# Nine of the 22 gate and up tiles of a feed-forward block from seven quarter products, with the high and low half of the input in one matmul

## The chip, the cores and the metric

The kernel runs on one core of a Trainium2 chip. The metric is the device time of one execution in microseconds (us); a kernel's time is the median of its runs. A core has a matrix engine (PE, with its weight loads shown apart as PEld), three other compute engines (DVE, ACT, POOL) and a queue that issues transfers (SP). Each engine runs its instructions in the order in which the program lists them, and waits for the results of others by semaphores.

## The reference, cut to what matters

Two layers, each a feed-forward block, a mixing block (convolution, a recurrent mixer, retention, attention) and a second feed-forward block; 512 tokens of width 1024, a hidden width of 2816. All is fp32.

```python
def swiglu(x, w_gate, w_up, w_down):
    return (jax.nn.silu(x @ w_gate) * (x @ w_up)) @ w_down

for l in range(DEPTH):                                   # DEPTH = 2
    x = x + 0.5 * swiglu(rmsnorm(x, ffn1_norm[l]), ffn1_w_gate[l], ffn1_w_up[l], ffn1_w_down[l])
    h = rmsnorm(x, mix_norm[l])
    ...                                                  # mixers on h @ w_in[l]
    x = x + jnp.concatenate([...], axis=-1) @ w_out[l]
    x = x + 0.5 * swiglu(rmsnorm(x, ffn2_norm[l]), ffn2_w_gate[l], ffn2_w_up[l], ffn2_w_down[l])
return rmsnorm(x, final_norm)
```

So there are four feed-forward blocks. The change touches their `x @ w_gate` and `x @ w_up`.

## The kernel before

Activations lie transposed: `x[d]` is a tile of 128 features by 512 tokens, for d = 0 to 7. An fp32 product is made of three reduced-precision ones (fp32r): each operand is split into a high part and a low part, and `mm3` (L336 to 340) adds high weight by high input (L338), high weight by low input (L339) and low weight by high input (L340). `norm_part` (L258) makes the two parts of the scaled input, `xg`: one tile of 128 x 2 x 512 for each d, high part first.

`ffn` (L343) goes through the hidden width in two halves of 11 tiles of 128. For each tile f it loads the gate and the up weights in one transfer of 1 MB into `w_raw` (a ring of two buffers), splits each of the two into `w_hi` (an ACT copy, L327) and `w_lo` (a DVE subtraction, L328), and makes two accumulations of 24 matmuls of 512 columns: `pg` (gate) and `pu` (up). `w_hi` and `w_lo` are rings of two buffers each, so that in steady work one is read by the gate matmuls and the other by the up matmuls, and a split can begin only when the matmuls that read the older content of its buffer are done. Behind the matmuls come, on other engines, `s = pg * rb` (DVE, L369), the silu (ACT, L370), `g = pu * s` (DVE, L372) and the split of g (ACT L374, DVE L375). After 11 tiles the down projection of that half follows, d = 0 to 7, with 33 matmuls each into `pd`.

PSUM has eight banks under three tags: `mm` (three: `pg` and others), `b` (three: `pu` and others) and `a` (two). The SBUF tiles of 512 columns have tag `f` (23 buffers), those of twice that tag `v` (19).

The order of the work on each engine is made when the program is built, by a list scheduler that follows a model of the engines' times: where several instructions of an engine could go, the one with the higher priority goes first, and priority is the place in the program. `split` runs under `high_priority(offset=AHEAD)`, which puts its instructions 4000 places ahead of where they stand.

Of the kernel before, what the change touches and what calls it, by code (L numbers as in the profile page):

```python
# [23 lines left out]
HALF = NF // 2  # L24
W = 256
AHEAD = 4000
PIECE = 512
MLA_TAGS = (("mm", "mm", "mm"), ("mm", "mm", "mm"), ("b", "a", "mm"), ("b", "a", "mm"))
H = 4
N = 64  # L30
C = 64
# [103 lines left out]
class K:  # L135
# [17 lines left out]
    def setup(self):  # L153
        tc, nc, I = self.tc, self.nc, self.I
        e = self.ctx.enter_context
        self.per = e(tc.tile_pool(name="per", bufs=1))
        self.ring = e(tc.tile_pool(name="ring", bufs=2))
        self.tmp = e(tc.tile_pool(name="tmp", bufs=2))
        self.psp = e(tc.tile_pool(name="ps", bufs=2, space=bass.MemoryType.PSUM))
        self.dr = e(tc.tile_pool(name="dr", bufs=2, space=bass.MemoryType.DRAM))  # L160
        per = self.per
        self.vec = per.tile([P, _vec_layout()], F32, name="vec")
        nc.sync.dma_start(self.vec, I["vec"])

        warm = self.tmp.tile([P, 1], F32, name="warm", bufs=1)
        nc.vector.memset(warm, 0.0)
        nc.scalar.activation(warm, warm, AF.Copy, scale=1.0)
        self.x = [self.ft(f"x{d}") for d in range(KD)]
        first = self.ring.tile([P, 2048], F32, name="w_raw", tag="w_raw", bufs=2)
        self.first = first  # L170
        for d in range(KD):
            nc.sync.dma_start(self.x[d], I["xT"][:, d, :])
            if d in (0, 3):
                q = 512 * (d // 3)
                nc.sync.dma_start(first[:, q:q + 512], I["gu1"][0, 0][:, q:q + 512])
        nc.sync.dma_start(first[:, 1024:2048], I["gu1"][0, 0][:, 1024:2048])
        self.con_t = per.tile([P, I["con"].shape[1]], F32, name="con_t")
        nc.sync.dma_start(self.con_t, I["con"])
        self.rc = per.tile([P, T], F32, name="rc")
        self.rs = per.tile([P, T], F32, name="rs")  # L180
        self.mt = per.tile([P, T], F32, name="mt")
# [76 lines left out]
    def norm_part(self, d, gain, l, square=True):  # L258

        nc, V, A = self.nc, self.nc.vector, self.nc.scalar  # L260
        x = self.x[d]
        if d == 0:
            self.acc = self.ft("acc")
            self.xh, self.xl, self.xo = [], [], []
        if gain == "final_norm":
            self.norm_square(d, True)
            o = self.ft("o")
            A.activation(o, x, AF.Copy, scale=self.v(gain, 0, d))
            self.xo.append(o)
            return  # L270
        hl = self.ht(f"xg{d}", dt=F32R)
        g = self.v(gain, l, d)
        A.activation(hl[:, 0], x, AF.Copy, scale=g)
        V.scalar_tensor_tensor(hl[:, 1], x, g, hl[:, 0].bitcast(F32), ALU.mult, ALU.subtract)  # L274
        self.xh.append(hl[:, 0])
        self.xl.append(hl[:, 1])
        if square:
            self.norm_square(d)
# [61 lines left out]
        T_.matmul(ps, lo, xh, start=False, stop=stop)  # L340


    def ffn(self, l, which, then, between=None):  # L343
        nc, V, A = self.nc, self.nc.vector, self.nc.scalar
        wgu, wdn = self.I[f"gu{which}"], self.I[f"dn{which}"]
        for half in range(2):
            gh, gl = [], []
            for f in range(HALF):
                raw, self.first = self.first, None
# [24 lines left out]
                A.copy(hl[:, 0], g)  # L374
                V.tensor_tensor(hl[:, 1], g, hl[:, 0].bitcast(F32), ALU.subtract)  # L375
                gh.append(hl[:, 0])
                gl.append(hl[:, 1])
            if between is not None:
                between()
                between = None  # L380
            for d in range(KD):
                raw = self.load(wdn[l, half, d], HALF * P)
                pd = self.ps("pd", "a")
                for a, b in ((0, 6), (6, HALF)):
                    hi, lo = self.split(raw[:, P * a:P * b], P * (b - a))
# [27 lines left out]
class Mixers:  # L413
# [44 lines left out]

    def x_back(self):
        k = self.k  # L460
        for d in range(0, KD, 2):
# [304 lines left out]
    def mla(self, j):  # L766
# [29 lines left out]

        po = k.ps("m_po", MLA_TAGS[2 * j + 1][2])

# [477 lines left out]
```

## Time and profile before

| | us |
|---|---|
| median of 3 runs | 2169.64 (2166.54 to 2171.83) |
| the profiled execution | 2169.86 |
| its span, first to last instruction | 2168.1 |
| PE busy in it | 2131.3 (98%) |
| DVE busy | 1113.3 (51%) |
| ACT busy | 711.6 (33%) |
| mean granted PE clock | 0.995 |

Busy times of PE overlap: matmuls are pipelined, and one that is shown with 390 ns starts 227 ns after the one before. What a matmul costs is therefore read from the distance of two starts, not from its length. "Idle before" a group, and what ended it, say who waited for whom.

### The profile page before, as it was taken

To read this page: it belongs to the slowest core of one execution; us is meant where nothing else is said; L and a number is where in the kernel's file an instruction comes from. 1 tells how busy PE (TensorE), PEld (TensorE's weight loads), DVE (VectorE), ACT (ScalarE), POOL (GpSimd) and SP (SyncE) were. 2 spreads that over 40 slices of the span, in tenths; PEclk is the share of its full clock that TensorE was granted. 3 is DMA by queue.
4 is the path that set the end of the run, shared out by engine and by line. 5 is a ranking of instruction groups with operands and counts; after the bars stand their busy time and mean duration, and the time that the engine had idled before them with its cause. 6 is when DMAs were issued, how large, how long until landed. Compare 5 with 4: busy or idle time off the path is not lost.

```text
span 2168.1 us, 27576 instructions
## 1 busy us (share of the span) xinstructions
PE 2131.3 (98%) x11316; PEld 1714.9 (79%) x11316; DVE 1113.3 (51%) x1917; ACT 711.6 (33%) x1061; POOL 122.4 (6%) x146
## 2 busy tenths in 40 slices
PE   8999999999999999999999999999999999999997
PEld 7888888788666888888888888887886578888886
DVE  4454445676577543443544444457756865434433
ACT  4222223443233422222322222335323243222232
POOL 2000001000020100000100000010001210000001
PEclk9999999999999999999999999999999999999998
DMA  4223224144002322322322232242330122223222
GB/s 170 97 85 106 98 95 151 61 118 129 20 21 86 116 98 85 117 97 79 106 97 91 94 109 95 92 147 72 116 101 21 64 90 105 91 80 111 97 87 79
DMA packets 65294, 204.68 MB, mean 94 GB/s; under 512 B 26512, under 2 KB 26768, under 8 KB 50960
## 3 DMA queue, kind: packets, MB, share of 16 engines
q1 hardware_dynamic: 65168, 202.93, 28.5%
q8 instruction: 88, 1.44, 0.3%
q14 instruction: 38, 0.31, 0.0%
HBM read 191.37 MB, written 9.44 MB: 93 GB/s over the span
## 4 chain that ended last, share of the span: by engine, by line
PE 93%; DVE 4%; ACT 1%; DMA 1%; issue 1%; SPq 0%; DVEq 0%; ACTq 0%
PE pg L338 7%; PE pg L340 7%; PE pg L339 7%; PE pu L338 7%; PE pd L340 7%; PE pu L339 7%; PE pd L339 7%; PE pd L338 7%; PE pu L340 7%; PE pj L338 4%; PE pj L339 4%; PE pj L340 4%; PE po L338 1%; PE po L339 1%; PE po L340 1%; PE m_pq L758 1%
## 5 line engine op out<-in xcount | busy, mean ns | idle before, releaser
L327 ACT CAST w_hi<-w_raw 128x1024 fp32r<-128x1024 f32 (+4 forms) x446 | 367.4, 836 | 1132.1 <-PE pg L339 308.9
L328 DVE TENSOR_TENSOR w_lo<-w_raw,w_hi 128x1024 fp32r<-128x1024 f32 (+4 forms) x446 | 425.7, 962 | 229.4 <-ACT w_hi L327 220.1
L338 PE MATMUL pg<-xg,w_hi 128*128 128x512 f32 x704 | 275.5, 391 | 6.2 <-ACT w_hi L327 6.2
L340 PE MATMUL pg<-xg,w_lo 128*128 128x512 f32 x704 | 275.0, 391 | 0.0
L339 PE MATMUL pg<-xg,w_hi 128*128 128x512 f32 x704 | 274.9, 390 | 0.0
L338 PE MATMUL pu<-xg,w_hi 128*128 128x512 f32 x704 | 274.1, 389 | 0.4 <-ACT w_hi L327 0.4
L339 PE MATMUL pu<-xg,w_hi 128*128 128x512 f32 x704 | 274.2, 389 | 0.0
L340 PE MATMUL pu<-xg,w_lo 128*128 128x512 f32 x704 | 273.9, 389 | 0.0
L340 PE MATMUL pd<-g,w_lo 128*128 128x512 f32 x704 | 273.9, 389 | 0.0
L338 PE MATMUL pd<-g,w_hi 128*128 128x512 f32 x704 | 273.9, 389 | 0.0
L339 PE MATMUL pd<-g,w_hi 128*128 128x512 f32 x704 | 273.9, 389 | 0.0
L372 DVE TENSOR_TENSOR g<-pu,s 128x512 f32<-128x512 f32 x88 | 60.9, 692 | 274.0 <-PE pu L340 271.2
L369 DVE TENSOR_TENSOR s<-pg,rb 128x512 f32<-128x512 f32 x88 | 60.8, 691 | 206.5 <-PE pg L340 206.4
L338 PEld LDWEIGHTS pg<-xg,w_hi 128*128 128x128 f32 x704 | 132.7, 188 | 33.7 <-ACT w_hi L327 6.2
L340 PEld LDWEIGHTS pg<-xg,w_lo 128*128 128x128 f32 x704 | 132.7, 188 | 28.5 <-DVE w_lo L328 1.0
L339 PEld LDWEIGHTS pg<-xg,w_hi 128*128 128x128 f32 x704 | 132.7, 188 | 28.0 <-DVE xg L274 0.5
L338 PEld LDWEIGHTS pu<-xg,w_hi 128*128 128x128 f32 x704 | 132.2, 188 | 28.1 <-ACT w_hi L327 0.9
L340 PEld LDWEIGHTS pu<-xg,w_lo 128*128 128x128 f32 x704 | 132.2, 188 | 27.5 <-DVE w_lo L328 0.2
L339 PEld LDWEIGHTS pd<-g,w_hi 128*128 128x128 f32 x704 | 132.2, 188 | 27.5
L338 PEld LDWEIGHTS pd<-g,w_hi 128*128 128x128 f32 x704 | 132.2, 188 | 27.4
L340 PEld LDWEIGHTS pd<-g,w_lo 128*128 128x128 f32 x704 | 132.2, 188 | 27.4
L339 PEld LDWEIGHTS pu<-xg,w_hi 128*128 128x128 f32 x704 | 132.2, 188 | 27.3
(294 smaller groups left out, 2706.5 us busy)
## 6 DMA issues: line engine op xcount, KB each, us to landing
w_raw<-gu SPq DMA_DIRECT2D x87, 1024.0 KB, 4.8
w_raw<-dn SPq DMA_DIRECT2D x64, 704.0 KB, 4.2
w_raw<-win SPq DMA_DIRECT2D x22, 1024.0 KB, 5.1
w_raw<-wo SPq DMA_DIRECT2D x32, 256.0 KB, 2.8
xs<-x SPq DMA_DIRECT2D x16, 256.0 KB, 4.7
x<-xs SPq DMA_DIRECT2D x16, 256.0 KB, 5.7
w_raw<-wtv SPq DMA_DIRECT2D x4, 576.0 KB, 4.2
x<-xT SPq DMA_DIRECT2D x8, 256.0 KB, 5.9
```

The costliest lines, as they stand in the source:

```text
L327: self.split_hi = self.nc.scalar.copy(hi[:, s], raw[:, s])
L328: self.nc.vector.tensor_tensor(lo[:, s], raw[:, s], hi[:, s].bitcast(F32), ALU.subtract)
L338: T_.matmul(ps, hi, xh, start=start, stop=False)
L339: T_.matmul(ps, hi, xl, start=False, stop=False)
L340: T_.matmul(ps, lo, xh, start=False, stop=stop)
L369: V.tensor_tensor(s, pg, rb, ALU.mult)
L372: V.tensor_tensor(g, pu, s, ALU.mult)
L758: mm(pq, wq[i][:, P * h:P * h + P], qa[i], start=i == 0, stop=i == 2)
```

## The change

Nine of the 22 gate and up tiles of each block (f = 3, 5, 7, 9 of the first half, f = 1, 3, 5, 7, 9 of the second; 36 tiles in all) are computed by a new function `seven`. It takes the pair of gate and up weights as a 2 x 2 block matrix (rows: gate or up; columns: the first and the last four of the eight feature tiles) and the input as another (the same feature halves by the first and the last 256 tokens), and forms the product from seven products of quarters instead of eight (the Winograd form of Strassen's method). Each quarter product is four feature tiles by 256 tokens. In it one matmul of 512 columns takes the high weight by the high and the low input side by side (two runs of 256 columns, into the two halves of a bank), and one of 256 columns takes the low weight by the high input into the first half; the two halves are added later.

What is new around it: `sums` makes the four input sums `T` once for each block, behind tile 0 (per pair of feature tiles two ACT copies, four DVE sums, and a split of each); `seven` makes the weight sums on DVE and splits seven quarters instead of four; three PSUM banks are used for the seven products (`y` takes four of them, `z` two, `x` one), with four ACT copies (`taken`) that read out partial results between the products; the combination is made on DVE. The weights arrive in three transfers instead of one. The other 13 tiles of a block, the down projection and the mixers stay.

```diff
+SEVEN = ((3, 5, 7, 9), (1, 3, 5, 7, 9))
+    def sums(self):
+        V, A = self.nc.vector, self.nc.scalar
+        ...
+        for i in range(KD // 2):
+            b = []
+            for d in (i, i + KD // 2):
+                t = self.ft("t_b")
+                A.activation(t, self.x[d], AF.Copy, scale=self.v(gain, l, d))
+                b.append((t[:, 0:256], t[:, 256:512]))
+            (b11, b12), (b21, b22) = b
+            ...
+            V.tensor_tensor(T1, b12, b11, ALU.subtract)
+            V.scalar_tensor_tensor(T2, b22, -1.0, T1, ALU.mult, ALU.subtract)
+            V.scalar_tensor_tensor(T3, b22, -1.0, b12, ALU.mult, ALU.subtract)
+            V.tensor_tensor(T4, T2, b21, ALU.add)
+            ...
+                for q in range(2):
+                    a = t[:, 256 * q:256 * q + 256]
+                    A.copy(hl[q][:, 0], a)
+                    V.tensor_tensor(hl[q][:, 1], a, hl[q][:, 0].bitcast(F32), ALU.subtract)
+
+    def seven(self, src, rb):
+        ...
+        raw = self.ring.tile([P, 2048], F32, name="w_raw", tag="w_raw", bufs=2)
+        nc.sync.dma_start(raw[:, 0:Q], src[:, 0:Q])
+        nc.sync.dma_start(raw[:, Q:3 * Q], src[:, 2 * Q:4 * Q])
+        nc.sync.dma_start(raw[:, 3 * Q:4 * Q], src[:, Q:2 * Q])
+        w22, w12 = raw[:, 2 * Q:3 * Q], raw[:, 3 * Q:4 * Q]
+        def parts(*srcs):
+            hi = self.ring.tile([P, 1152], F32R, name="w_hi", tag="w_hi", bufs=2)
+            lo = self.ring.tile([P, 1152], F32R, name="w_lo", tag="w_lo", bufs=2)
+            ...
+                A.copy(hi[:, z], t)
+                V.tensor_tensor(lo[:, z], t, hi[:, z].bitcast(F32), ALU.subtract)
+        with self.tc.high_priority(offset=AHEAD):
+            w11, = parts(raw[:, 0:Q])
+            V.tensor_tensor(raw[:, 0:2 * Q], raw[:, 0:2 * Q], raw[:, Q:3 * Q], ALU.subtract)
+            r2, r4 = self.ft("w_s2"), self.ft("w_s4")
+            V.scalar_tensor_tensor(r2, raw[:, 0:Q], -1.0, w22, ALU.mult, ALU.subtract)
+            V.tensor_tensor(r4, w12, r2, ALU.add)
+            S1, S2 = parts(raw[:, Q:2 * Q], r2)
+            S4, S3 = parts(r4, raw[:, 0:Q])
+            w22, w12 = parts(raw[:, 2 * Q:4 * Q])
+        y, x, z = self.ps("f_y", "mm"), self.ps("f_x", "b"), self.ps("f_z", "b")
+        ...
+        def product(ps, w, b, start):
+            hi, lo = w
+            for i in range(4):
+                c = slice(P * i, P * i + P)
+                nc.tensor.matmul(ps.rearrange("p (q t) -> p q t", q=2), hi[:, c], b[i], start=start and i == 0,
+                                 stop=False, skip_group_check=True)
+                nc.tensor.matmul(ps[:, 0:256], lo[:, c], b[i][:, 0], start=False, stop=i == 3, skip_group_check=True)
+        def taken(ps):
+            t = self.ft("f_m")
+            A.copy(t, ps)
+            return t
+        product(y, w11, tok(0, 0), True)
+        m1 = taken(y)
+        product(z, S1, T(1), True)
+        m5 = taken(z)
+        product(y, S2, T(2), False)
+        u2 = taken(y)
+        product(z, S4, tok(1, 1), False)
+        product(y, S3, T(3), False)
+        u3 = taken(y)
+        product(x, w12, tok(1, 0), True)
+        product(y, w22, T(4), False)
+        ...                                  # the combination: 9 DVE operations, a silu and a copy on ACT
     def ffn(self, l, which, then, between=None):
         ...
             for f in range(HALF):
+                if f in SEVEN[half]:
+                    g = self.seven(wgu[l, half * HALF + f], rb)
+                    ...                      # the split of g, as in the other tiles
+                    continue
         ...
+                if f == 0 and half == 0:
+                    self.sums()
```

## Rows read from the trace of the kernel before

**Rows 1.** The page, engines: busy time, share, instructions; the chain that ended last.

```profile
PE 2131.3 (98%) x11316; PEld 1714.9 (79%) x11316; DVE 1113.3 (51%) x1917; ACT 711.6 (33%) x1061; POOL 122.4 (6%) x146
PE 93%; DVE 4%; ACT 1%; DMA 1%; issue 1%; SPq 0%; DVEq 0%; ACTq 0%
```

**Rows 2.** Groups by line and shape: busy us, mean ns; idle before, releaser.

```profile
L338 PE MATMUL pg<-xg,w_hi 128*128 128x512 f32 x704 | 275.5, 391 | 6.2 <-ACT w_hi L327 6.2
...
L328 DVE TENSOR_TENSOR w_lo<-w_raw,w_hi 128x1024 fp32r<-128x1024 f32 x174 | 215.1, 1236 | 74.8 <-ACT w_hi L327 65.7
...
L639 DVE TENSOR_TENSOR ret_ms<-ret_ps,ret_big 128x256 f32<-128x256 f32 x32 | 11.5, 418 | 0.1
...
L1100 ACT COPY ch<-psT 128x256 f32<-128x256 f32 x28 | 9.8, 373 | 39.6 <-PE psT L1099 31.4 <-DVE sm L783 3.9 <-PE m_ptp L793 3.3
...
L794 ACT COPY m_pT<-m_ptp 128x512 f32<-128x512 f32 x16 | 9.4, 587 | 8.4 <-PE m_ptp L793 8.4
```

**Rows 3.** Timeline of PE, first matmuls of two neighbouring gate and up tiles.

```profile
98.73 0.39 PE L338 MATMUL pg<-xg,w_hi 128*128 128x512 f32 x1
98.95 0.39 PE L339 MATMUL pg<-xg,w_hi 128*128 128x512 f32 x1
...
109.61 0.39 PE L338 MATMUL pg<-xg,w_hi 128*128 128x512 f32 x1
```

**Rows 4.** Timeline of PE in a projection with 256 columns.

```profile
416.28 0.28 PE L502 MATMUL pn<-w_hi,xg 128*128 128x256 f32 x1
416.40 0.28 PE L503 MATMUL pn<-w_lo,xg 128*128 128x256 f32 x1
416.52 0.28 PE L504 MATMUL pn<-w_hi,xg 128*128 128x256 f32 x1
```

**Rows 5.** Timeline at a tile's end: its last matmuls, then ACT and DVE.

```profile
109.15 0.39 PE L339 MATMUL pu<-xg,w_hi 128*128 128x512 f32 x1
...
109.64 1.05 ACT L327 CAST w_hi<-w_raw 128x1024 fp32r<-128x1024 f32 x1 [3.87 <-PE pu L339]
...
109.88 0.69 DVE L372 TENSOR_TENSOR g<-pu,s 128x512 f32<-128x512 f32 x1 [3.38 <-PE pu L340]
...
110.60 0.62 ACT L374 CAST g<-g 128x512 fp32r<-128x512 f32 x1
...
110.72 1.23 DVE L328 TENSOR_TENSOR w_lo<-w_raw,w_hi 128x1024 fp32r<-128x1024 f32 x1
```

**Rows 6.** Timeline where splits and a PSUM copy compete for ACT.

```profile
491.68 0.39 PE L340 MATMUL pj<-xg,w_lo 128*128 128x512 f32 x1
491.88 1.14 ACT L327 CAST w_hi<-w_raw 128x512 fp32r<-128x512 f32 x2 [3.01 <-PE pj L339]
...
492.93 0.58 ACT L572 COPY ro_r<-pj 128x512 f32<-128x512 f32 x1
```

**Rows 7.** Timeline of PE between two links of the recurrent chain (zy).

```profile
602.52 0.55 PE L793 MATMUL m_ptp<-con_t,m_p 128*128 128x128 f32 x3
...
603.00 0.78 PE L1123 MATMUL zy<-ch,Gm 128*64 128x64 f32 x16
```

**Rows 8.** Timeline: the end of an ACT operation and the matmul that waited for it.

```profile
613.88 0.19 ACT L786 ACTIVATION_READ_ACCUMULATOR m_p<-m_sc,sm,m_fqa 128x1 f32 x1
...
614.13 0.44 PE L793 MATMUL m_ptp<-con_t,m_p 128*128 128x128 f32 x2 [0.17 <-ACT m_p L786]
```

**Rows 9.** Busy time by stretch: one gate and up tile; a stretch of the mixers.

```profile
98.73:109.61 10.88, 10.88 (x50) 9.01 (x48) 4.44 (x5) 3.17 (x4) 0.00 (x0) 1.00 0.29 96
...
595.00:610.00 15.00, 14.27 (x153) 10.39 (x152) 11.10 (x28) 7.52 (x17) 2.12 (x4) 1.00 0.01 2
```

(The columns: PE, PEld, DVE, ACT, POOL busy us with instruction counts, granted clock, DMA share, GB/s.)

**Rows 10.** DMA issues: count, KB of each, median us to landing.

```profile
w_raw<-gu SPq DMA_DIRECT2D x87, 1024.0 KB, 4.8
...
w_raw<-wo SPq DMA_DIRECT2D x32, 256.0 KB, 2.8
```

**Rows 11.** Timeline of PE in the kernel's first matmuls.

```profile
9.42 0.63 PE L338 MATMUL pg<-xg,w_hi 128*128 128x512 f32 x1
9.85 0.63 PE L339 MATMUL pg<-xg,w_hi 128*128 128x512 f32 x1
```

More of the change, by code (lines that the diff above doesn't have):

```diff
@@ L168, in setup @@
         self.x = [self.ft(f"x{d}") for d in range(KD)]
+        self.x_moved = False
         first = self.ring.tile([P, 2048], F32, name="w_raw", tag="w_raw", bufs=2)
@@ L263, in norm_part @@
             self.acc = self.ft("acc")
-            self.xh, self.xl, self.xo = [], [], []
+            self.xh, self.xl, self.xo, self.xhl = [], [], [], []
+            self.gain = (gain, l)
         if gain == "final_norm":
@@ L274, in norm_part @@
         V.scalar_tensor_tensor(hl[:, 1], x, g, hl[:, 0].bitcast(F32), ALU.mult, ALU.subtract)
+        self.xhl.append(hl)
         self.xh.append(hl[:, 0])
@@ L340, in mm3 @@
         T_.matmul(ps, lo, xh, start=False, stop=stop)
+    def sums(self):
+        V, A = self.nc.vector, self.nc.scalar
+        self.T = []
+        gain, l = self.gain
+        for i in range(KD // 2):
[5 more added lines that the diff above has]
+            (b11, b12), (b21, b22) = b
+            s = [self.ft("t_s") for _ in range(2)]
+            T1, T2, T3, T4 = (t[:, 256 * q:256 * q + 256] for t in s for q in range(2))
+            V.tensor_tensor(T1, b12, b11, ALU.subtract)
+            V.scalar_tensor_tensor(T2, b22, -1.0, T1, ALU.mult, ALU.subtract)
+            V.scalar_tensor_tensor(T3, b22, -1.0, b12, ALU.mult, ALU.subtract)
+            V.tensor_tensor(T4, T2, b21, ALU.add)
+            out = []
+            for t in s:
+                if len(self.T) < 2 or not self.x_moved:
+                    hl = self.vt("T", shape=(P, 2, 2, 256), dt=F32R)
+                    hl = [hl[:, q] for q in range(2)]
+                else:
+                    hl = [self.ft("T", shape=(P, 2, 256), dt=F32R) for q in range(2)]
+                for q in range(2):
+                    a = t[:, 256 * q:256 * q + 256]
+                    A.copy(hl[q][:, 0], a)
+                    V.tensor_tensor(hl[q][:, 1], a, hl[q][:, 0].bitcast(F32), ALU.subtract)
+                out += hl
+            self.T.append(out)
@@ new lines, in seven, with fold @@
+    def seven(self, src, rb):
+        nc, V, A = self.nc, self.nc.vector, self.nc.scalar
+        Q = 512
+        raw = self.ring.tile([P, 2048], F32, name="w_raw", tag="w_raw", bufs=2)
[6 more added lines that the diff above has]
+            lo = self.ring.tile([P, 1152], F32R, name="w_lo", tag="w_lo", bufs=2)
+            a = 0
+            for t in srcs:
+                z = slice(a, a + t.shape[1])
+                A.copy(hi[:, z], t)
+                V.tensor_tensor(lo[:, z], t, hi[:, z].bitcast(F32), ALU.subtract)
+                a = z.stop
+            return [(hi[:, q:q + Q], lo[:, q:q + Q]) for q in range(0, a, Q)]
+        with self.tc.high_priority(offset=AHEAD):
[8 more added lines that the diff above has]
+        y, x, z = self.ps("f_y", "mm"), self.ps("f_x", "b"), self.ps("f_z", "b")
+        tok = lambda h, j: [t[:, :, 256 * j:256 * j + 256] for t in self.xhl[4 * h:4 * h + 4]]
+        T = lambda n: [t[n - 1] for t in self.T]
+        def product(ps, w, b, start):
[20 more added lines that the diff above has]
+        product(y, w22, T(4), False)
+        s, g = self.ft("s"), self.ft("g")
+        def fold(o, t):
+            V.tensor_tensor(o, t[:, 0:256], t[:, 256:512], ALU.add)
+        V.tensor_tensor(u2, z, u2, ALU.add)
+        fold(s[:, 256:512], u2)
+        V.tensor_tensor(u3, u3, m5, ALU.add)
+        fold(g[:, 256:512], u3)
+        V.tensor_tensor(m1, x, m1, ALU.add)
+        fold(s[:, 0:256], m1)
+        V.tensor_tensor(s, s, rb, ALU.mult)
+        A.activation(s, s, AF.Silu)
+        A.copy(g[:, 0:256], y[:, 256:512])
+        V.tensor_tensor(g[:, 0:256], y[:, 0:256], g[:, 0:256], ALU.add)
+        V.tensor_tensor(g, g, s, ALU.mult)
+        return g
@@ L348, in ffn @@
             for f in range(HALF):
+                if f in SEVEN[half]:
+                    g = self.seven(wgu[l, half * HALF + f], rb)
+                    hl = self.vt(f"g{f}", dt=F32R)
+                    A.copy(hl[:, 0], g)
+                    V.tensor_tensor(hl[:, 1], g, hl[:, 0].bitcast(F32), ALU.subtract)
+                    gh.append(hl[:, 0])
+                    gl.append(hl[:, 1])
+                    continue
                 raw, self.first = self.first, None
@@ L460, in x_back @@
         k = self.k
+        k.x_moved = True
         for d in range(0, KD, 2):
```

## The prediction

> **What bounds the kernel now.** I read the engines' busy times and the chain that ended last first: PE is busy 98% of the span and makes up 93% of the chain [rows 1]. Then the groups by line: the gate matmuls waited 6.2 us in all, and that is the kernel's start [rows 2]. So PE's time is the kernel's time, and a column taken from PE is worth its full price as long as PE finds the next operand ready. Third, the timeline, since a matmul's length hides its cost: two neighbouring gate and up tiles start 10.88 us apart [rows 3], which is 48 matmuls at 0.2267 us. Fourth, the stretch of one tile: DVE is busy 4.44 and ACT 3.17 of 10.88 us [rows 9]; each has some 6 us to spare, and that cover is what the change draws on.
>
> **What it removes: matmul columns.** A 256-column matmul with a weight load of its own starts 0.120 us after the one before [rows 4]; with 0.2267 us for 512 columns, both are the columns at 2.4 GHz plus 0.013 us. A quarter product is four pairs of 512 and 256 columns: 4 x (0.2267 + 0.120) = 1.387 us; seven are 9.71 us against 10.88, so 1.17 us less for each of 36 tiles: 42.2 us. No row shows a 512-column matmul that reads its input in two runs; the nearest prices are one of 512 (0.2267) and two of 256 (0.240). I take the first; the second would add 28 x 0.0133 = 0.37 us a tile, 13.4 us in all.
>
> The Trainium skill, page "TensorE: Matmul & The Clock Gate", section "Back-to-back issue gap", gives an isolated gap of columns / 2.4 GHz plus 2.5 ns; by that estimate a tile would save 1.26 us and the change 45.4 us. The trace shows more per matmul (0.2267 and 0.120 us), and my sum uses the trace.
>
> **What it adds on PE: three waits on one bank.** `y` takes four products, and before each later one ACT must have copied the bank out. Each such copy has one product (1.387 us) of cover. Whether that is enough depends on what stands ahead of it on ACT, which works in order. Two rows decide. First, after a projection ends, ACT does both pieces of the next weight split (0.525 us each) and only then the copy out of PSUM [rows 6]: splits come free earlier and have priority. `seven` keeps that: a buffer of `w_hi` comes free 0.49 us after the start of the last matmul that read it (109.15 to 109.64 [rows 5]), which in the new order is about 0.14 us after a product ends, while the last results are there about 0.26 us after it. So at the end of each `y` product a split is ready just ahead of the copy. Second, PE goes on about 0.06 us after the ACT operation it waits for ends (613.88 + 0.19 to 614.13 [rows 8]). A copy of 512 from PSUM takes 0.58 us [rows 2, 6], a split of 1024 occupies ACT for 0.96 us (109.64 to 110.60 [rows 5]).
>
> I walk one new tile, time 0 at its first matmul, taking the tile before it as an ordinary one.
> - First wait. ACT from 0.04: splits of S1 and S2 to 1.09, the previous tile's g to 1.62; by then the buffer of w11 is free (1.53), so the splits of S4 and S3 to 2.67; then m1's copy to 3.24. PE has finished S1's product at 2.77 and starts S2's at 3.30. Idle 0.53 us; no other operand is ready. (S1's low part lands within 0.13 us of when it is wanted, which is inside this wait.)
> - Second wait. S2 ends at 4.69; the split of w22 and w12 holds ACT from 4.83 to 5.79; u2's copy ends at 6.37. S4's product ends at 6.07, S3's can start at 6.43: 0.36 us. The order on PE is made by readiness, at the grain of single matmuls: three transposes of the attention, which stands later in the program, fill a gap of the recurrent chain, which then goes on at once [rows 7]. So w12's first high matmul (0.23 us) goes in; idle 0.13 us.
> - Third wait. S3 ends at 7.82, the rest of w12 at 8.98. The next tile's gate split holds ACT from 7.96 to 8.92, u3's copy ends at 9.50, `y` is free at 9.56: 0.58 us. The gate's first two matmuls fit in from 9.18 (its high part lands at 9.01); idle 0.20 us, and w22's product runs from 9.63 to 11.02.
> Idle is 0.53 + 0.13 + 0.20 = 0.86 us. A tile takes 9.71 + 0.86 = 10.57 us, 0.31 less than now. Over 36 tiles the waits cost 31.0 us. The bounds: zero, if the copies go first, and 0.53 + 0.36 + 0.58 = 1.47 us (52.9 us in all), if nothing fills. I take 0.86 because rows 6 and rows 7 show both halves of it at work in this kernel.
>
> **What it adds elsewhere, costed at nothing.**
> - DVE in a new tile: 13 operations of 512 at a distance of 0.61 us (0.69 long, overlapped), two of 1024 at 1.14 (1.24 long [rows 2]) and four of 256 at 0.45 (0.42 long [rows 2]): some 12 us, more than the tile itself. It is covered by the ordinary tile beside it: 12 + 4.44 = 16.5 us of a pair's 21.4. New tiles never stand next to each other. The combination at a tile's end feeds only the down projection, and the weight sums need the raw weights alone; they run in the 5.4 us before the tile, beside one 0.69 us operation. Without that cover the price would be DVE's excess, 1.4 us a tile.
> - ACT: five splits of 512, one of 1024, four copies, a silu, a copy of 256 (0.37 [rows 2]) and g's split, some 7.1 us in the tile; hidden but for the waits above.
> - `sums`: 32 DVE operations of 256 (14.4 us) and 24 on ACT (some 9 us) for each block, between tile 0 and tile 3. Two ordinary tiles leave DVE 12.9 us, tile 0 some more; the splits keep priority and now have 3.9 us to spare [rows 5]. Zero, and at most the missing 1.5 us by four: 6 us.
> - Loads: the buffer is held until w12's low part is made, 7.2 us into the tile, and its next content is wanted 16 us into it. 1 MB lands in 4.8 us; three pieces at 2.8 us one after another would be 8.4 [rows 10]. Hidden by either; SP issues three for one and has nothing else queued in these stages.
>
> **The sum**, against the profiled execution (2169.86 us: 2168.1 of span and 1.8 around it, 0.2 above the median): 2169.86 - 42.2 + 31.0 = 2158.7, so 2158.5 for the median. The forecast's own spread is 0.2 us a tile: 2151 to 2166.
>
> **Rivals.**
> - Slower: the waits stay bare. The order on PE is fixed when the program is built; if the gaps are not seen there (the model has a copy ending earlier than it does), nothing is put into them and each tile waits 1.47 us. That is 0.30 us above the saving: 36 x 0.30 = 10.7, 2180.4. It decides from 1.17 us of idle time a tile. For it: three waits a tile on a queue that is 7.1 of 10 us full. Against: rows 7. Chance 0.25.
> - The copies go ahead of the splits, or the first one does: splits have 1.4 us or more to spare at each place, so the waits vanish: 2127.5; if only the first goes, 36 x 0.53 = 19 us less than the forecast, 2139.5. Against: rows 6. Chance 0.16.
> - The saving isn't there in full: the two-run matmuls cost as two of 256, 13.4 us above the forecast, 2171.9. Against: the two sizes shown cost by their columns alone [rows 3, 4]; nothing speaks for it but that no row shows the form. Chance 0.06.
> - PE's clock falls for the gaps. At the kernel's start 512 columns take 0.43 us, the 1.2 GHz level [rows 11]; if the 36 tiles ran so, each would take some 9 us more, 2480 in all. Against: the mixers' stretch with 0.73 us idle in 15 us, gaps as long as these, was granted 1.00 throughout [rows 9]. Chance 0.01. The Trainium skill, same page, section "A second HAM failure mode: psum-queue depth-cycling", tells of just such small gaps between groups that let the clock fall back; this case's trace does not show it.
>
> **How the numbers follow.** The forecast has 0.52. A measurement of this kernel tells a change of about 0.3% (6.5 us) from none. Faster by more: 0.44 of the forecast (below 2163.1) and 0.16 of the copies first: 0.60. Within: the rest of the forecast, the two-run case, and a little of the bare waits: 0.16. Slower: 0.24. The range reaches from the first wait gone (2139) to the bare waits with a little of what I cost at nothing (2183); outside lie the case without any wait, the clock, and a stack of the dear bounds.
>
> **What would show it.** In the new trace: PE starts 0.347 us apart per pair of a 512 and a 256 matmul (0.36 would be the two-run case); a new tile 10.4 to 10.8 us long; PE idle before S2's product for m1's copy, about 0.5 us, with ACT's splits of S4 and S3 just ahead of that copy; one `x` matmul and two of the next gate placed ahead of `y` products; DVE busy some 16 us a pair, with nothing waiting for the combination. It is wrong if the idle time before `y` products is near zero or near 1.5 us a tile, or if PE waits for weight sums, for T or for loads.

## The result, and the profile after

The change made the kernel slower: 2253.16 us (median of 4 runs, 2251.06 to 2255.95) against 2169.92, a ratio of 1.0386 (1.0368 to 1.0404). The forecast was 2158.5 us in a range that ended at 2183.

The page of the kernel after, its engines (busy us, share, instructions) and the chain that ended last; they answer to [rows 1]:

```profile
PE 2153.9 (96%) x11604; PEld 1708.5 (76%) x11604; DVE 1419.4 (63%) x2549; ACT 911.1 (40%) x1481; POOL 123.6 (5%) x146
...
PE 82%; DVE 7%; ACT 7%; DMA 1%; issue 1%; SPq 1%; DVEq 0%; ACTq 0%
```

PE is no longer the whole chain: 93% became 82%, and DVE and ACT have 14% between them. So PE now waits for operands. The list of waits says for which (waiter, releaser: us in total, times, longest):

```profile
PEld f_y L426 <- ACT f_m L432: 39.1, 72, 6.1
PEld f_z L428 <- DVE w_lo L405: 27.7, 36, 1.2
PEld f_z L426 <- ACT f_m L432: 24.5, 32, 0.8
...
PEld f_z L426 <- DVE T L384: 7.6, 6, 3.4
```

The first is a wait for a copy out of the bank `y`, of the kind that the prediction had counted. The second, once in each of the 36 tiles, is for the low part of a weight sum, which it had costed at nothing. The third is for the copy out of the bank `z`, which it had not counted: its three waits were all on `y`. The fourth is for the input sums `T`. Where they lie is seen by stage. Windows: a second half before (block 2), then after the first halves of blocks 1 and 2, the second half of block 2 and the mixers of layer 1 (columns as in [rows 9]):

```profile
901.97:1021.65 119.68, 119.68 (x530) 99.13 (x528) 48.52 (x55) 34.23 (x43) 0.00 (x0) 1.00 0.27 92
...
5.99:150.05 144.06, 130.61 (x576) 102.50 (x577) 96.67 (x165) 73.09 (x121) 10.90 (x7) 0.94 0.30 105
...
743.17:877.66 134.49, 124.52 (x577) 100.26 (x576) 93.29 (x158) 64.94 (x107) 3.14 (x2) 0.97 0.25 82
937.50:1061.83 124.33, 120.02 (x570) 96.38 (x569) 84.78 (x125) 56.48 (x88) 0.00 (x0) 1.00 0.27 88
1500.24:1856.34 356.10, 345.04 (x2448) 260.73 (x2446) 240.72 (x544) 135.56 (x244) 35.87 (x52) 0.98 0.26 79
```

The same four stages took 125.20, 121.74, 119.68 and 347.00 us before. In a second half nothing but new and ordinary tiles happens, six of them ordinary at 10.88 us [rows 3], so a steady new tile takes (124.33 - 6 x 10.88) / 5 = 11.81 us: not 10.57 as forecast, and 0.93 more than the tile it replaces. Three of a first half's four new tiles are such steady ones; what is left of a first half's loss belongs to tile 3, the first that uses `T`: 9.8 to 10.2 us in blocks 2 to 4, and 16.1 in block 1, where 1.4 of it already lies in tile 0 (15.13 us from its first matmul to that of tile 1, 13.78 before). So the spans differ by

| | us |
|---|---|
| 32 steady new tiles, 0.93 each | 29.8 |
| the first new tile of each block: 16.1 + 10.0 + 10.2 + 9.8 | 46.1 |
| mixers, which the change doesn't touch: -0.6 and +9.1 | 8.5 |
| sum (the two spans, 2252.3 and 2168.1, differ by 84.2) | 84.4 |

**A steady tile.** (S1 to S4 are the weight sums, as four of the seven left operands; m1, u2 and u3 are the copies of `y` behind its first three products, m5 is the copy of `z`.) Timeline of after, DVE ahead of a new tile and in it (start, length):

```profile
944.47 1.22 DVE L411 TENSOR_TENSOR w_raw<-w_raw 128x1024 f32<-128x1024 f32 x1
948.65 0.69 DVE L501 TENSOR_TENSOR g<-pu,s 128x512 f32<-128x512 f32 x1 [2.96 <-PE pu L344]
949.26 0.68 DVE L413 SCALAR_TENSOR_TENSOR w_s<-w_raw 128x512 f32<-128x512 f32 x1
949.86 0.68 DVE L405 TENSOR_TENSOR w_lo<-w_raw,w_hi 128x512 fp32r<-128x512 f32 x1
950.46 0.68 DVE L414 TENSOR_TENSOR w_s<-w_raw,w_s 128x512 f32<-128x512 f32 x1
```

The same, PE:

```profile
948.38 0.39 PE L426 MATMUL f_y<-xg,w_hi 128*128 128x512 f32 x1
...
949.78 0.40 PE L426 MATMUL f_z<-T,w_hi 128*128 128x512 f32 x1
950.60 0.39 PE L428 MATMUL f_z<-T,w_lo 128*128 128x256 f32 x1 [0.42 <-DVE w_lo L405]
...
952.71 0.49 PE L426 MATMUL f_z<-xg,w_hi 128*128 128x512 f32 x1 [0.44 <-ACT f_m L432]
953.04 0.35 PE L428 MATMUL f_y<-T,w_lo 128*128 128x256 f32 x1
```

And ACT:

```profile
950.45 0.61 ACT L404 CAST w_hi<-w_s 128x512 fp32r<-128x512 f32 x1
950.97 0.58 ACT L432 COPY f_m<-f_y 128x512 f32<-128x512 f32 x1
951.45 0.62 ACT L404 CAST w_hi<-w_s 128x512 fp32r<-128x512 f32 x1
952.07 0.59 ACT L432 COPY f_m<-f_z 128x512 f32<-128x512 f32 x1
```

DVE makes the first difference of raw weights at 944.47, is idle for 2.96 us, and makes the sums `r2` (L413) and `r4` (L414) only behind `g` of the tile before (L501), after the new tile has begun at 948.38. Nothing in the data says so: L413 needs L411's result and the raw weights. All that follows is late: the low part of S1 (made at 949.86; PE waits for it at 950.60), the split of `r2` on ACT at 950.45, and behind it in ACT's queue the copies of m1 and m5 (952.07, for which PE waits at 952.71, in a matmul of S4's product that was put ahead of the rest of S2's). A matmul's length is more than its distance to the next, so the idle times of 0.42 and 0.44 us understate the two waits: by the distances of the starts they cost 0.59 and 0.61 us.

**The first new tile of a block.** Timeline of after in block 2, ACT and then DVE:

```profile
766.14 0.63 ACT L499 ACTIVATE s<-s 128x512 f32<-128x512 f32 x1 [3.16 <-DVE s L498]
...
768.01 1.33 ACT L364 ACTIVATE t_b<-x,vec 128x512 f32<-128x512 f32 x2
...
766.81 0.69 DVE L501 TENSOR_TENSOR g<-pu,s 128x512 f32<-128x512 f32 x1 [0.70 <-ACT s L499]
...
786.58 0.69 DVE L501 TENSOR_TENSOR g<-pu,s 128x512 f32<-128x512 f32 x1
787.19 0.68 DVE L413 SCALAR_TENSOR_TENSOR w_s<-w_raw 128x512 f32<-128x512 f32 x1
```

ACT again, then PE:

```profile
787.90 0.62 ACT L404 CAST w_hi<-w_s 128x512 fp32r<-128x512 f32 x1
788.43 0.58 ACT L432 COPY f_m<-f_y 128x512 f32<-128x512 f32 x1
...
789.06 0.79 PE L426 MATMUL f_y<-T,w_hi 128*128 128x512 f32 x1 [5.76 <-ACT f_m L432]
...
790.23 0.63 PE L426 MATMUL f_y<-T,w_hi 128*128 128x512 f32 x1
790.66 0.41 PE L428 MATMUL f_y<-T,w_lo 128*128 128x256 f32 x1
```

A window of 4 us behind that wait:

```profile
789.90:793.90 4.00, 4.00 (x13) 3.42 (x14) 1.34 (x2) 1.65 (x3) 0.00 (x0) 0.50 0.02 4
```

The input sums begin (ACT L364, 768.01) only behind tile 0's `s` and `g` (766.14, 766.81), though their inputs are there since the block began and ACT was idle for 3.16 us just before; `g` of tile 2 comes behind the input sums (786.58), `r2` behind that (787.19), m1's copy behind `r2`'s split in ACT's queue (788.43), and PE has waited 5.76 us. Then it runs at a granted clock of 0.50, the 1.2 GHz level: a matmul of 512 columns and the next start 0.43 us apart (790.23, 790.66), as at the kernel's start [rows 11].

**The mixers.** Their program is the same. In the traces each engine's order of instructions in layer 0 is that of before as well; in layer 1 it is not. ACT before, then after:

```profile
1532.05 1.25 ACT L327 CAST w_hi<-w_raw 128x576 fp32r<-128x576 f32 x2 [5.42 <-PE pj L339]
...
1537.56 1.04 ACT L960 COPY Nb<-Lb 64x1024 f32<-64x1024 f32 x1 [3.19 <-DMA Lb<-s]
...
1599.23 1.04 ACT L1092 COPY Nb<-Lb 64x1024 f32<-64x1024 f32 x1 [11.70 <-DMA Lb<-s]
1600.30 1.25 ACT L331 CAST w_hi<-w_raw 128x576 fp32r<-128x576 f32 x2
```

In after a copy waits 11.70 us for its transfer, and the weight split behind it in the queue, which PE wants, waits with it. Before the change this copy stood behind that split.

### The profile page after: what moved, and what is told of

Read it like the earlier page. It is cut to its first block, busy times and chain, and to the rows that moved or that the text cites. A ratio compares the mean times of both kernels' runs of the same rounds, so it can differ in the third digit from the quotient of the medians.

```text
span 2252.3 us, 29571 instructions
## 1 busy us (share of the span) xinstructions
PE 2153.9 (96%) x11604; PEld 1708.5 (76%) x11604; DVE 1419.4 (63%) x2549; ACT 911.1 (40%) x1481; POOL 123.6 (5%) x146
## 4 chain that ended last, share of the span: by engine, by line
PE 82%; DVE 7%; ACT 7%; DMA 1%; issue 1%; SPq 1%; DVEq 0%; ACTq 0%
PE pd L342 7%; PE pd L344 7%; PE pd L343 7%; PE f_y L426 5%; PE pg L342 4%; PE pu L342 4%; PE pu L343 4%; PE pg L344 4%; PE pg L343 4%; PE pu L344 4%; PE pj L342 3%; PE pj L344 3%; PE pj L343 3%; PE f_y L428 3%; ACT w_hi L404 2%; PE f_z L426 2%
## 5 line engine op out<-in xcount | busy, mean ns | idle before, releaser
L331 ACT CAST w_hi<-w_raw 128x512 fp32r<-128x512 f32 (+2 forms) x374 | 291.6, 794 | 683.0 <-PE pd L343 269.1
L332 DVE TENSOR_TENSOR w_lo<-w_raw,w_hi 128x512 fp32r<-128x512 f32 (+2 forms) x374 | 336.7, 909 | 236.1 <-ACT w_hi L331 236.0
L426 PE MATMUL f_y<-T,w_hi 128*128 128x512 f32 x432 | 165.9, 413 | 21.4 <-ACT f_m L432 21.4
L342 PE MATMUL pg<-xg,w_hi 128*128 128x512 f32 x416 | 167.8, 403 | 6.1 <-ACT w_hi L331 6.0
L343 PE MATMUL pg<-xg,w_hi 128*128 128x512 f32 x416 | 163.7, 394 | 0.2 <-DVE xg L277 0.2
L342 PE MATMUL pu<-xg,w_hi 128*128 128x512 f32 x416 | 162.1, 390 | 0.5 <-ACT w_hi L331 0.5
L343 PE MATMUL pu<-xg,w_hi 128*128 128x512 f32 x416 | 162.2, 390 | 0.0
L405 DVE TENSOR_TENSOR w_lo<-w_raw,w_hi 128x512 fp32r<-128x512 f32 (+1 forms) x144 | 117.5, 818 | 70.6 <-ACT w_hi L404 70.6
L344 PE MATMUL pu<-xg,w_lo 128*128 128x512 f32 x416 | 162.0, 389 | 0.0
L344 PE MATMUL pj<-xg,w_lo 128*128 128x512 f32 x368 | 144.7, 395 | 1.7 <-DVE w_lo L332 1.7
L342 PE MATMUL pj<-xg,w_hi 128*128 128x512 f32 x368 | 145.1, 394 | 0.5 <-ACT w_hi L331 0.5
L343 PE MATMUL pj<-xg,w_hi 128*128 128x512 f32 x368 | 144.5, 393 | 0.0
L428 PE MATMUL f_y<-T,w_lo 128*128 128x256 f32 x432 | 126.2, 292 | 0.2 <-DVE w_lo L405 0.2
```

The costliest lines, as they stand in the source:

```text
L331: self.split_hi = self.nc.scalar.copy(hi[:, s], raw[:, s])
L332: self.nc.vector.tensor_tensor(lo[:, s], raw[:, s], hi[:, s].bitcast(F32), ALU.subtract)
L342: T_.matmul(ps, hi, xh, start=start, stop=False)
L343: T_.matmul(ps, hi, xl, start=False, stop=False)
L405: V.tensor_tensor(lo[:, z], t, hi[:, z].bitcast(F32), ALU.subtract)
L426: nc.tensor.matmul(ps.rearrange("p (q t) -> p q t", q=2), hi[:, c], b[i], start=start and i == 0, stop=False, skip_group_check=True)
```

## The experiments

**The theory, A.** `r2` and `r4` take SBUF buffers of tag `f`, as do `s` and `g` of every tile and the `t_b` and `t_s` of the input sums. Buffers of one tag are handed out in the order of the program. The weight sums have priority, but no buffer until the `s` and `g` of the tile before have theirs, and those wait for PE; likewise the input sums wait behind tile 0's `s` and `g`, which wait for the norm. **Rivals:** B, the copies behind splits on ACT are what is long; C, DVE has too much to do. Four kernels tell them apart.

**Weight sums in buffers of their own** (all edits are to the kernel after):

```diff
-    NV, NFS = 19, 23
+    NV, NFS = 19, 21
-            r2, r4 = self.ft("w_s2"), self.ft("w_s4")
+            r2, r4 = [self.ring.tile([P, 512], F32, name=n, tag=n, bufs=1) for n in ("w_s2", "w_s4")]
```

> The changed kernel, with the two weight sums r2 and r4 in two SBUF buffers of their own instead of the pool of tag f (which has 21 buffers instead of 23 to make room). Theory A (buffers of a tag are handed out in program order, so r2 and r4 wait until the s and g of the tile before, which come earlier in the program, have theirs): the weight sums now run ahead of the tile, the waits of PE for S1's low part (0.59 us a tile) and for m5's copy behind the late S2 (0.61 us) vanish, a steady new tile takes 10.6 to 10.9 us instead of 11.82, the second halves of the four blocks are about 5 us shorter each, and the whole takes 2205 to 2225 us. Theory B (ACT's queue: copies behind splits) has the same copies in the same places: 2245 to 2255. Theory C (DVE simply has too much to do): the sums move but as much is late elsewhere, 2245 to 2260.

Measured: 2222.97 us, as theory A expected, 30 less, although the mixers came out 11.5 us longer than in after (354.3 and 362.3); the gate and up stages are 39.3 us shorter. DVE ahead of a new tile:

```profile
935.57 1.22 DVE L411 TENSOR_TENSOR w_raw<-w_raw 128x1024 f32<-128x1024 f32 x1
936.83 0.69 DVE L413 SCALAR_TENSOR_TENSOR w_s<-w_raw 128x512 f32<-128x512 f32 x1
937.56 0.69 DVE L414 TENSOR_TENSOR w_s<-w_raw,w_s 128x512 f32<-128x512 f32 x1
939.76 0.69 DVE L501 TENSOR_TENSOR g<-pu,s 128x512 f32<-128x512 f32 x1 [1.50 <-PE pu L344]
```

The window of the second half of block 2:

```profile
928.61:1047.26 118.65, 117.54 (x569) 96.43 (x568) 85.69 (x125) 55.36 (x88) 0.00 (x0) 1.00 0.28 92
```

The sums now stand right behind L411, ahead of `g`, in DVE's idle time. A new tile takes (118.65 - 65.28) / 5 = 10.67 us. C falls for the steady tile: DVE does the same work, and the sums are in time. B falls as the cause of these 1.14 us: no copy was moved ahead of a split.

**Input sums earlier in the program:**

```diff
                 if f == 0 and half == 0:
+                    self.sums()
                     self.norm_sum()
...
-                if f == 0 and half == 0:
-                    self.sums()
```

> The changed kernel, with the call of sums() moved up in the program, from behind g of tile 0 to ahead of its s; nothing else. Theory A: the buffers of tag f for the input sums are then handed out before those of tile 0, 1 and 2's s and g, which wait for the norm; the input sums are made during tiles 0 and 1 and tile 3 no longer waits for T, nor for weight sums stuck behind it; each first half is 8 to 12 us shorter (the first block's 15 or more, since the clock no longer falls there), the steady tile stays at 11.82 us, the whole takes 2205 to 2220 us. Theory C (DVE and ACT have too much to do between tile 0 and tile 3): it stays within 8 us of 2253.

Measured: 2226.22 us, 27 less, and 6 above what theory A expected. The first half of block 2:

```profile
740.81:867.05 126.24, 122.34 (x578) 98.56 (x576) 92.87 (x158) 65.28 (x108) 3.17 (x2) 1.00 0.27 88
```

It is 8.2 us shorter than in after, and its clock is 1.00 instead of 0.97. The second half stays (124.35). In block 1 only 1.9 us were won (142.2 against 144.1), against 15 expected; that is taken up below. This edit moves the call's place in the program, and with it its priority as well as its turn for buffers, and no run gave the input sums buffers of their own. That it is the buffers is therefore argued and not shown: in after ACT was idle for 3.16 us ahead of 766.14, and a lower priority alone does not keep an operation off an idle engine.

**Both edits:**

> Both edits: the weight sums in buffers of their own, the input sums ahead of tile 0's s in the program. Theory A: the two gains add up, 2165 to 2185 us; what is left above the forecast of 2158.5 is the mixers of layer 1 (9 us more than before the change) and the waits for ACT's copies. Theory B: above 2235. Theory C: above 2245.

Measured: 2186.00 us, 67 less than after and 1 above the expected range (ratio to before 1.0069, 1.0054 to 1.0084). The two gains add up: the gate and up stages got 39 us shorter in the first run, 28 in the second and 69 in this one. Some 16 us above before are left: the first half of block 1 takes 137.44 us (125.20 before), the mixers 351.7 and 355.2 (349.7 and 347.0); a new tile takes 10.68.

**Priority for the copies:**

```diff
-            A.copy(t, ps)
+            with self.tc.high_priority(offset=2 * AHEAD):
+                A.copy(t, ps)
```

> As the run with both edits, and the four copies out of PSUM between the products have priority over the weight splits on ACT. If the remaining waits of PE (0.86 us a new tile in the forecast) come from the splits that stand ahead of the copies, they nearly vanish: 25 to 31 us less than with both edits alone, 2135 to 2160. If the splits are what is late instead, once they stand behind the copies, no gain or a loss: within 5 us of the run with both edits, or above it.

Measured: 2185.34 us, the same. ACT there:

```profile
929.87 0.61 ACT L404 CAST w_hi<-w_raw 128x512 fp32r<-128x512 f32 x1
930.39 0.58 ACT L433 COPY f_m<-f_y 128x512 f32<-128x512 f32 x1
```

The copy still stands behind the split, as in the run with both edits. By the prediction's estimates the first of the two splits ahead of it is ready some 0.1 us earlier, and priority chooses among what is ready; why the second one (929.87) stayed ahead too is not shown. The order did not change, so this run says nothing on what the order costs.

**The copies first in fact:** ACT's splits of S4 and S3, of w22 and w12, and of the next tile's gate are queued behind the copies of m1, u2 and u3 (kernel with both edits).

```diff
 ...
+        def behind(*srcs):
+            with self.tc.issue_after(self.take.ins), self.tc.high_priority(offset=AHEAD):
+                return parts(*srcs)
         m1 = taken(y)
+        S4, S3 = behind(r4, raw[:, 0:Q])
 ...
         u2 = taken(y)
+        w22, w12 = behind(raw[:, 2 * Q:4 * Q])
 ...                                                # and in split, for the tile behind:
+        order, self.take = self.take, None
+            if order is not None:
+                e.enter_context(self.tc.issue_after(order.ins))
```

> As the run with both edits (2186.0), and in program the splits of S4 and S3, of w22 and w12, and of the next gate tile are queued on ACT behind the copies of m1, u2 and u3. The run that only gave the copies a higher priority left ACT's order as it was, since a split is ready some 0.1 us before the copy. If the waits that are left (0.27 us at the first y copy, and some 0.4 us around the fillers and the restarts behind them) come from the splits ahead of the copies, a new tile goes from 10.68 to 9.8 to 10.1 us: 20 to 31 us less, 2155 to 2166. If PE waits for the splits instead, once they are last (S4 or w22's high part): no gain, 2180 or more.

Measured: 2190.96 us. The expectation failed. A new tile takes 10.52 us (second halves 117.9), 0.16 less and not 0.6 to 0.9; the rest moved to another wait, and the mixers came out 6 us longer. Its list of waits:

```profile
PE f_x L431 <- DVE w_lo L410: 12.3, 35, 0.4
```

The waits for copies are gone from the steady tiles (four are left, in first tiles), and PE waits in 35 tiles for the low part of w12, which stands behind the split that now comes later.

**The mixers, first try:** Nb's copy on POOL instead of ACT (kernel with both edits).

```diff
-                A.copy(Nb[64:128], Lb[64:128, ::-1])
+                G.tensor_copy(Nb[64:128], Lb[64:128, ::-1])
```

> As the run with both edits (2186.0), and in the mixers one copy (Nb from Lb, 64 x 1024) runs on POOL instead of ACT. In the trace of that run the copy stands on ACT ahead of the second half of a weight split, and waits 12.3 us for its transfer, so that the projection pn waits 5.4 us; in the kernel before it stands behind that split. If that order alone is what the mixers of the two layers lost (351.7 and 355.2 us against 349.7 and 347.0), they are back at 347 to 351 us and the whole takes 2174 to 2180. If it is something else (buffers, transfers), it stays within 3 us of 2186.

Measured: 2195.78 us; the expectation failed. The wait of `pn` is gone, but the mixers take 359.9 and 359.3 us: with one instruction moved, the whole order of the mixers came out another. So this run does not tell what the one copy costs; a later one settles more.

**The first block, input sums behind tile 1's gate split,** with all edits so far but the bare priority:

```diff
+                if begin:
+                    raw = self.load(wgu[l, 1], 2048)
+                    self.pre = raw, self.split(raw[:, 0:1024], 1024)
+                    with self.tc.issue_after(self.split_hi.ins), self.tc.issue_after(self.split_lo.ins):
+                        self.sums()
```

> All of these (weight sums in buffers of their own, input sums early, splits behind the copies, Nb's copy on POOL), and in the first block the input sums are queued on ACT and DVE behind tile 1's gate split, which is put ahead of them in the program. With the input sums early, the first block's tiles 0 and 1 wait 3.7 us for a low part behind operations that take 1.3 to 1.5 us instead of 0.41 while POOL adds up squares, and PE's clock is granted at 0.85 for a while. If that is why the first half is 137.4 us there against 125.2 before the change, it becomes 125 to 131 us, and the whole 2140 to 2156. If not, the first half stays above 134 and the whole above 2152.

Measured: 2174.83 us, 19 above the expected range. The first half of block 1 takes 131.50 us, just outside what was expected; with the copies first alone it took 135.81, so 4.3 of the 5.9 us against 137.44 are this edit's. What was wrong there is seen in the run with both edits: DVE, then POOL, then PE.

```profile
20.46 1.33 DVE L370 SCALAR_TENSOR_TENSOR t_s<-t_b,t_s 128x256 f32<-128x256 f32 x1
21.72 1.50 DVE L371 SCALAR_TENSOR_TENSOR t_s<-t_b 128x256 f32<-128x256 f32 x1
...
28.23 0.41 DVE L369 TENSOR_TENSOR t_s<-t_b 128x256 f32<-128x256 f32 x1
...
18.78 6.97 POOL L292 TENSOR_TENSOR acc<-acc,sq 128x512 f32<-128x512 f32 x5
...
26.89 0.80 PE L344 MATMUL pg<-xg,w_lo 128*128 128x512 f32 x1 [3.55 <-DVE w_lo L332]
```

The window from 17 to 28 us of that run:

```profile
17.00:28.00 11.00, 7.00 (x28) 5.16 (x27) 8.17 (x7) 9.03 (x16) 8.28 (x7) 0.85 0.24 90
```

And of this one:

```profile
17.00:28.00 11.00, 10.19 (x46) 7.95 (x44) 7.93 (x6) 8.80 (x16) 9.29 (x7) 1.00 0.23 92
```

While POOL adds up the squares (five operations in 6.97 us, up to 25.75), a DVE operation of 256 columns takes 1.33 or 1.50 us; at 28.23 it takes 0.41. The split that PE wants stood behind such operations. In this run it stands ahead of them, and the clock is 1.00 instead of 0.85.

**One more ordinary tile ahead of the first new one** (f = 4, 6, 8, 10 in the first halves):

> As the last, with f = 4, 6, 8, 10 instead of 3, 5, 7, 9 as the new tiles of the first halves, one more ordinary tile behind the input sums. If time for the input sums is still short between tile 0 and tile 3, the first half of the first block gains 3 us or more over the last run. The last tile's combination (some 5 us behind its last product) is then wanted at the down projection's eleventh step, 7 us in: no wait from that. In all 0 to 6 us less than the last run; more only if the down projection waits.

Measured: 2193.49 us, 19 more than the last run and not 0 to 6 less, since the mixers came out at 360.1 and 362.7. The first half of block 1 gained what was expected, 4.0 us (127.5); the others 0.6 to 0.7.

**The mixers, settled:** the weight sums in PSUM, tag `f` with 23 buffers again (kernel with both edits).

```diff
-            r2, r4 = self.ft("w_s2"), self.ft("w_s4")
+            r2, r4 = self.ps("w_s2", "a"), self.ps("w_s4", "a")
```

> As the run with both edits (2186.0), but the weight sums r2 and r4 lie in the two PSUM banks of tag a, free in these stages, and tag f keeps its 23 SBUF buffers. With 21 the order of the mixers' instructions is another than before the change; with this it is the same, instruction for instruction, as in the kernel before. If the mixers' 10.2 us over the kernel before come from that order (two buffers fewer, in stages that the change does not touch), they take 349.7 and 347.0 us again, the rest stays, and the whole takes 2174 to 2179. If the change itself makes the mixers longer (a clock, transfers), 2183 to 2188.

Measured: 2177.55 us (ratio 1.0023, 1.0013 to 1.0032). The mixers take 346.8 and 350.1 us, 696.9 together; before the change 696.7. ACT at the place shown for after:

```profile
1538.56 1.25 ACT L331 CAST w_hi<-w_raw 128x576 fp32r<-128x576 f32 x2 [5.43 <-PE pj L343]
...
1545.57 1.04 ACT L1091 COPY Nb<-Lb 64x1024 f32<-64x1024 f32 x1 [4.69 <-DMA Lb<-s]
```

The copy stands behind the split again, and in the trace every engine has the order of before in both layers. So have the mixers of the run below with all that helped, which take 348.0 and 349.4 us; so they do not get longer by seven products in the stages beside them. Layer 1 takes 350.1 and 349.4 us in that order, 356.1 in the order of after: the order costs it some 6 us. The other 3 of its 9.1 us are not explained by the order: in the order of before, layer 0 took 346.8 to 349.7 us from run to run, and layer 1 347.0 to 350.1. A new tile takes 10.62 us: own buffers of another kind give the same as in the first run, so it was the buffers.

**All that helped, together,** and w12 split ahead of w22 in a piece of its own:

```diff
 ...
-        w22, w12 = behind(raw[:, 2 * Q:4 * Q])
+        w12, w22 = behind(1, w12, w22)
 ...
```

> All that helped, together: weight sums in PSUM, input sums early and in the first block behind tile 1's gate split, splits behind the copies, w12 split ahead of w22 in a piece of its own (the x product waited 0.51 us for the low part of the two together), f = 4, 6, 8, 10 in the first halves, f = 1, 3, 5, 7 in the second halves of the two blocks ahead of the mixers and 1, 3, 5, 7, 9 in the other two (34 new tiles), which leaves the order of the mixers as before the change. If the 0.51 us goes too, a new tile takes 9.9 to 10.1 us, the second halves 115 to 117 us, and the whole 2143 to 2155. If another wait takes its place, as the low part did when the copies went first, second halves of 118 and 2158 to 2168.

Measured: 2168.11 us (ratio 0.9981, 0.9971 to 0.9991). The second case came true: second halves of 118.2, the wait moved once more, 33 times:

```profile
PE pg L350 <- DVE w_lo L338: 12.6, 33, 0.8
```

Now it is the next tile's gate: its split, behind u3's copy, is one piece of 1024, and its low part stands on DVE behind two operations of the combination.

**That split in two pieces of 512,** the new tiles f = 3, 5, 7, 9 and 1, 3, 5, 7, 9 again; and beside it the same with 4, 6, 8, 10 in the first half of block 1:

```diff
-                        self.split(raw[:, 1024 * o:1024 * o + 1024], 1024, 512 if begin else 1024)
+                        self.split(raw[:, 1024 * o:1024 * o + 1024], 1024,
+                                   512 if begin or o == 0 and self.take is not None else 1024)
```

> As the run with all that helped (2168.1), but the gate weights of the tile behind a new tile are split in two pieces of 512 instead of one of 1024, and the new tiles are f = 3, 5, 7, 9 and 1, 3, 5, 7, 9 in all blocks again (36). In that run each tile behind a new one waited 0.55 + 0.11 us for the gate's low part, whose subtraction of 1024 stood on DVE behind two operations of the combination. If a piece of 512 is ready between them, the wait goes, a new tile takes 9.9 to 10.1 us, and the second halves take 115 to 116 us instead of 118.2; the mixers of layer 1 have the order of the changed kernel, not that of before (347 to 357 us). The whole: 2147 to 2162. If the wait only moves once more, second halves of 117.5 to 118.5 and 2163 to 2178.

> As the run beside it, with f = 4, 6, 8, 10 in the first half of the first block alone. If the input sums still come late for tile 3 there (first half 131.5 us with f = 3, 127.5 with f = 4 in earlier runs), it is 2 to 4 us shorter than the run beside it; if not, the two agree within 2 us.

Measured: 2153.82 us (ratio 0.9919, 0.9900 to 0.9937) and 2150.58 us (0.9905, 0.9884 to 0.9925). The second half of block 2 in the latter:

```profile
896.21:1011.09 114.88, 114.88 (x569) 96.93 (x568) 87.04 (x135) 56.23 (x98) 0.00 (x0) 1.00 0.30 95
```

PE is busy throughout, and a new tile takes (114.88 - 65.28) / 5 = 9.92 us, 0.96 less than an ordinary one. The first half of block 1 takes 129.09 and 125.67 us, 3.4 apart; of these 1.4 are lost again in the down projection behind it (61.2 us instead of 59.8), which now follows a new tile. Against before, the gate and up stages are 26 us shorter and the mixers, in an order like that of after, 6 longer. So the method is worth 20 us here, once the operands are there in time.

## Why the prediction was wrong

- **The matmuls: right.** Four pairs start 1.40 us apart in after (948.38 to 949.78), 1.387 was forecast and 1.44 in the two-run case. The rest, 0.013 by seven, is 0.09 us a tile.
- **The fillers: right.** One `x` matmul and two of the next gate stand ahead of `y` products, as walked.
- **"The weight sums need the raw weights alone; they run in the 5.4 us before the tile": this step failed.** They need a buffer too, and in after they were made inside the tile, behind `g` of the tile before. I looked at what feeds an operation and at how busy its engine is, not at where its result goes. Two runs that gave them other buffers took the tile from 11.81 to 10.67 and 10.62 us. Over the 32 steady tiles the step cost some 37 us (1.14 each). The wait for m5's copy out of `z`, which the prediction has no term for, went with it.
- **`sums` "zero, and at most 6 us": failed, by what looks like the same cause.** It cost some 45 us in four first tiles: sums begun only behind tile 0's `s` and `g`, weight sums stuck behind them, a copy stuck behind a split. Block 1 lost most; there tile 0's `g` stands at 42.98 us, 2.6 us ahead of tile 3's first matmul, and in block 2 11.1 us ahead. The prediction priced DVE's time between tile 0 and tile 3, not when the sums could begin. The prediction's list of what would show it wrong named a wait for weight sums or for T; both came.
- **The first wait and those that remain: nearly right.** With the buffers mended a tile took 10.62 to 10.68 us against 10.57 forecast; the waits were shorter than walked (by the distances of the starts, in the run with both edits, 0.38 us for m1, 0.04 for u2, none for u3, instead of 0.53, 0.13 and 0.20). Three restarts behind waits and fillers (0.1 us each, below), 0.08 us for S1's low part and the 0.09 of the pairs, none of them priced, made up for it. So the total is near in part by luck.
- **The rival "the copies go first, 2127.5" was mis-sized.** I had the waits vanish with the order. In the run that did it the tile fell by 0.16 us only, since w12's low part was late next, and then the gate's. Three orders had to be mended, one after the other, to get to 9.92; at each I had asked what the copies cost, not what stands behind them.
- **The rival "slower" had the wrong mechanism.** It was about bare waits on copies; its 2180.4 is far below what came. That the change is slower was given 0.24, and it came by a path that the prediction held for free.
- **The clock, given 0.01 as a case for all tiles, fell among the new tiles in the first ones only,** where PE waited several us. In the second halves, where PE is idle 4.3 of 124.3 us in waits like the 0.42 and 0.44 us shown, it is 1.00. The Trainium skill, page "TensorE: Matmul & The Clock Gate", section "A second HAM failure mode: psum-queue depth-cycling", tells of small idle times between groups that make the clock fall; these rows do not show it.
- **Not forecast at all: 8.5 us in the mixers,** stages that the diff does not touch. Some 6 us of layer 1's 9.1 are another order of their instructions.

With both losses mended and the mixers in their old order, 2177.55 is still 19 above the forecast: 14 of it is the first half of block 1 (138.2 against 124.0), 3 the other gate and up stages; the rest lies mainly between the profiled run (2176.13) and the median. Of those 14, the 4.3 us of the split behind DVE operations slowed beside POOL are the part that was shown; the slowed operations come with the input sums' earlier place, and are not among the losses of after. Not settled: why the mixers, in the very order of before, take 2.9 us less in layer 0 and 3.1 more in layer 1; and why, in block 1, tile 0 takes 1.4 us more in after, where a weight split (10.59 us) waits 0.91 us for its transfer and before did not.

## What to carry to other kernels

Price an added operation by what it reads, what it writes to and what stands ahead of it in every queue: a result that takes its buffer from a pool shared with later work of the tile before came late here, whatever its priority. When a wait is taken away by reordering, walk on to the next operand in that queue before counting the gain. And see in the trace that stages outside the diff kept their order, since a scheduler that reorders them can hide or feign several us.

## What the runs showed of the hardware that I had not expected

- DVE operations with two inputs in SBUF took 1.33 and 1.50 us instead of 0.41 while POOL added up tiles in SBUF. The Trainium skill, page "SBUF — State Buffer", section "Who interferes with whom", says that a DVE instruction with two SBUF inputs contends with a GpSimd instruction that reads SBUF, and calls the port pair that they share an exclusive lock. The trace agrees: a POOL operation of that group is 1.33 us in the mean, and the two DVE operations each end some 0.3 us behind the end of one (21.51 and 22.93).
- A matmul that had to wait puts off the next one too: behind the wait at 952.71 in after, the next starts 0.33 us later (953.04), not 0.23. With the wait gone, this goes as well; in the run with both edits three such restarts are some 0.3 us of a tile.
- Behind the wait of 5.76 us the granted clock was 0.50 in the 4 us shown. So that wait cost more than its length.
